# Layer 0 of a two-layer hybrid block: projections and neighbourhood attention as two stages, or as one in two token phases

## The chip, the cores and the metric

The kernel runs on one core of one Trainium2 chip, as one program with one launch. The metric is the device time of one execution in microseconds (us). The kernel before takes 3484.09 us, the median of 3 runs (3483.88 to 3485.11).

## The reference

The block works on 2048 latent tokens and 256 context tokens of 1024 numbers, in float32. Layer 0 is 2-D neighbourhood attention: latent tokens stand on a grid of 32 rows by 64 columns, and each of 16 heads (64 numbers each) lets a query see a window of 8 rows by 16 columns, with a learned bias for the relative position, and all 256 context tokens, in one softmax. Context tokens see the context alone.

```python
h = modulate(x, norm_w, shift, scale)            # rms norm, adaLN
q, k, v, z = jnp.split(h @ w_in, 4, axis=-1)     # w_in: 1024 x 4096
hc = modulate(xc, norm_w, shift_c, scale_c)
qc, kc, vc, zc = jnp.split(hc @ w_in, 4, axis=-1)
s_loc = q . k (window) * dh ** -0.5 + bias       # -inf outside the window
s_ctx = q . k_ctx * dh ** -0.5
p = softmax([s_loc, s_ctx]);  o = p_loc @ v + p_ctx @ v_ctx
x = x + gate * ((o * silu(z)) @ w_out)           # and the same for the context
```

Layer 1 is a gated linear recurrence in both directions, with projections of its own, and a final norm. The change doesn't touch it.

## The kernel before, in words

Full float32 precision is kept by splitting: a number is the sum of a part that the fast float32r product takes (hi) and the exact rest (lo). A projection is three products, hi hi, hi lo and lo hi (`mm3`, L207 to L213).

**Stage 1, `layer0_in`, L216.** The normalised tokens are built transposed and split, in five groups: four of 512 latent tokens and one of 256 context tokens (`GROUPS`). All five stay on chip. The 32 blocks of 128 weight columns (8 each of q, k, v, z; one block is one pair of heads) are loaded once, split by ScalarE and GpSimd, and multiplied with all five groups. q, k and z are written transposed (128 columns of the pair on the partitions, tokens along the row): the weights stand still and 512 tokens stream. Values are wanted with tokens on the partitions: `v_product` holds 128 tokens still and streams 256 value columns (L374). q and k go to DRAM as hi and lo (`split_out`), z with its SiLU (`gate_out`). In the middle, beside the blocks of pairs 1 to 3, stand the bias tables (`bias_tables`, L399) and the sums of adaLN parameters by lanes (`ada_lanes`, `ada_sum`): one of eight sums behind each weight block.

**Stage 2, `attention`, L479.** Pair after pair of heads; of each pair four groups of 8 query rows (`ROWG`; they read 12, 16, 16 and 12 key rows), then the context's queries; of each row group four bands of 16 query columns. I call one pair, row group and band a unit. For a unit and a head: scores into a PSUM tile `s` of two banks (two buffers); VectorE adds the bias table and takes the minimum (L494; scores are kept with their sign turned); ScalarE takes the exponential and its sum (L496); VectorE scales (L499); TensorE transposes in chunks of 128 into `tps` (L509, three banks), which ScalarE, or at each sixth turn VectorE (`EV = "aaaaav"`), copies out (L513, L515); TensorE multiplies with the values of the pair (L522), each head's 64 output rows in one half of the bank `o_ps`; a product of float32 without the split is two instructions in the trace. Scores (L596, L599, L615) stack hi and lo of q on the 128 partitions of one tile (`pair_tile`, L451), and k hi twice or k lo twice under them: two products on 128 rows give all that is wanted. So each of k hi and k lo is loaded twice. Everything is read back from DRAM: q, keys, values (16 loads a pair), tables and z.

**Stage 3, `layer0_out`, L678.** The output projection: both halves of the output weights (64 KB a partition split, `out_weights`) and 18 tiles of 128 tokens. Then layer 1.

**What sets the order.** The program is written for a planner that simulates the engines' times: it orders each engine's instructions beforehand, by what is ready and, among that, by place in the program. `after` adds an order between two instructions of one engine. Nearly all DMAs are issued by SyncE in one order; a tile that takes the place of older tiles waits for those that it overlaps (`reuse_waits="tile"`).

Of the kernel before, what the change touches and what calls it, by code (L numbers as in the profile page):

```python
# [13 lines left out]
ALU = mybir.AluOpType  # L14
# [11 lines left out]
# scores are kept with their sign turned  # L26
# [7 lines left out]
KBLOCKS = [(0, 12), (12, 8), (20, 12)]  # L34
KPARTS = [((0, 0, 12),), ((0, 4, 8), (1, 0, 8)), ((1, 0, 8), (2, 0, 8)), ((2, 0, 12),)]
# [4 lines left out]
TPS = 3  # L40
EV = "aaaaav"
TEB = 6
PB = 4
PCB = 3
# column bands whose context keys are weighted together
# [8 lines left out]
class Core:  # L54
# [71 lines left out]
    def ada_start(self, pool, psum, tag, tag2):  # L126
        """shift and scale of layer 0 from whole rows of weights: shift by lanes, scale on TensorE."""
# [37 lines left out]
    def rsqrt(self, y, x, pool):  # L165
        """y = x ** -0.5 for positive x, by Newton steps from a guess off the exponent."""
# [11 lines left out]
    def norms(self, xts, pool, small, tag="junk"):  # L178
        """1 / rms of the rows of each tile, one column each."""
# [36 lines left out]
    def layer0_in(self):  # L216
        nc, tc, I, S = self.nc, self.tc, self.I, self.S
        with ExitStack() as st:
            pp = st.enter_context(tc.tile_pool(name="l0p", bufs=1, reuse_waits="tile", space=PSUM))

            class PsPool:
                def tile(self, shape, dt, name, tag):
                    return pp.tile(shape, dt, name=name, tag=tag, bufs=4 if tag == "mm" else 3)
            ps = PsPool()
            ha = st.enter_context(tc.tile_pool(name="l0ha", bufs=1, reuse_waits="tile"))
            hi, lo = [], []

            def tokens(pool, g):
                n = GROUPS[g][1]
                hi.append(pool.tile([P, NDC, n], F32R, name=f"hi{g}"))  # L230
                lo.append(pool.tile([P, NDC, n], F32R, name=f"lo{g}"))
            for g in range(3):
                tokens(ha, g)
            wk = st.enter_context(tc.tile_pool(name="l0k", bufs=2, reuse_waits="tile"))
            sx = ExitStack()
            xp = sx.enter_context(tc.tile_pool(name="l0x", bufs=4, reuse_waits="tile", side="right"))
            sm = st.enter_context(tc.tile_pool(name="l0s", bufs=4, reuse_waits="tile"))

            def weights(cg, wh, wl):
                raw = wk.tile([P, NDC, P], F32, name="wraw", tag="wraw", bufs=1)  # L240
                m = nc.sync.dma_start(out=raw, in_=I["w0"][cg])
                if cg in (0, 8, 24):
# [3 lines left out]

            def granule(cg, pool=wk, **kw):
                wh = pool.tile([P, NDC, P], F32R, name="wh", tag="wh", **kw)
                wl = pool.tile([P, NDC, P], F32R, name="wl", tag="wl", **kw)
                weights(cg, wh, wl)  # L250
                return wh, wl

            def split_out(cg, p, t0, n, dst_h, dst_l, keys):
                oh = wk.tile([P, 512], F32R, name="oh", tag="oh")
                ol = wk.tile([P, 512], F32R, name="ol", tag="ol")
                ohv, olv, pv = oh[:, :n], ol[:, :n], p[:, :n]
                if not keys and n == 512:
                    ohv, olv = (custom(t, [[-16, 8], [P, 4], [1, 16]], 7 * 16) for t in (oh, ol))
                    pv = p.rearrange("p (r j c) -> p r j c", r=8, j=4)
                if keys:  # L260
                    nc.scalar.mul(out=ohv, in_=pv, mul=KSCALE)
                    nc.vector.scalar_tensor_tensor(olv, pv, KSCALE, ohv.bitcast(F32), ALU.mult, ALU.subtract)
                else:
                    nc.scalar.copy(out=ohv, in_=pv)
                    nc.vector.tensor_sub(olv, pv, ohv.bitcast(F32))  # L265
                r = slice(cg * P, (cg + 1) * P)
                nc.sync.dma_start(out=dst_h[r, t0:t0 + n], in_=oh[:, :n].bitcast(F32))
                nc.sync.dma_start(out=dst_l[r, t0:t0 + n], in_=ol[:, :n].bitcast(F32))

            def gate_out(cg, p, t0, n):  # L270
                sg = wk.tile([P, 512], F32, name="sg", tag="oh")
                nc.scalar.activation(sg[:, :n], p[:, :n], AF.Sigmoid)
                z = wk.tile([P, 512], F32, name="zo", tag="ol")
                nc.vector.tensor_mul(z[:, :n], p[:, :n], sg[:, :n])
                nc.sync.dma_start(out=S["z"][cg * P:(cg + 1) * P, t0:t0 + n], in_=z[:, :n])

            def q_out(pr):
                return lambda p, t0, n: split_out(pr, p, t0, n, S["qh"], S["ql"], False)

            def k_out(pr):  # L280
                return lambda p, t0, n: split_out(pr, p, t0, n, S["kh"], S["kl"], True)

            def z_out(pr):
                return lambda p, t0, n: gate_out(pr, p, t0, n)

            def x_load(g, xrs):
                t0, n, cond = GROUPS[g]
                for i, xt in enumerate(xrs):
                    src = I["ctx"][i * P:(i + 1) * P, :] if cond else I["x"][t0 + i * P:t0 + (i + 1) * P, :]
                    m = nc.sync.dma_start(out=xt, in_=src)  # L290
                    self.after(m, self.last_dma)
                    self.last_dma = m
                return xrs

            def x_tiles(g):
                return x_load(g, [xp.tile([P, D], F32, name="xt", tag="xt") for _ in range(GROUPS[g][1] // P)])

            def normalise(xrs):
                for i in range(0, len(xrs), 2):
                    rs = self.norms(xrs[i:i + 2], xp, sm)  # L300
# [3 lines left out]
            def build(g, xrs):  # L304
                self.build_hT(xrs, hi[g], lo[g], 0, GROUPS[g][2], 0, HalfPool(xp, 2), ps, "tp", "hf")

            with tc.tile_pool(name="l0a", bufs=1, reuse_waits="tile") as ap:
                self.ada_inputs(ap)
                ada = self.ada_start(ap, ps, "mm", "tp")
                next(ada)  # L310
                x0 = x_load(0, [ap.tile([P, D], F32, name=f"x0{i}") for i in range(4)])
                next(ada)
                self.ada_done(0)
                normalise(x0)
                first = [(granule(0), q_out(0)), (granule(8), k_out(0)), (granule(24, xp, bufs=1), z_out(0))]
                x1 = x_tiles(1)
                build(0, x0)
                next(ada)
            hb = st.enter_context(tc.tile_pool(name="l0hb", bufs=1, reuse_waits="tile"))
            tokens(hb, 3)  # L320
            x2 = [hb.tile([P, 2, D], F32, name=f"x2{i}", tag=f"t4{i}") for i in range(2)]
            x2 = x_load(2, [x2[i // 2][:, i % 2] for i in range(4)])

            def product(w, g, evac):
                t0, n, _ = GROUPS[g]
                wh, wl = w
                p = ps.tile([P, 512], F32, "mm", "mm")
                m = self.mm3(p[:, :n], lambda dc: wh[:, dc, :], lambda dc: wl[:, dc, :],
                             lambda dc: hi[g][:, dc, :], lambda dc: lo[g][:, dc, :])
                evac(p, t0, n)  # L330
                return m

            def token_product(cg, evac):
                w = granule(cg)
                return [product(w, g, evac) for g in range(len(GROUPS))][-1]

            def granules(pr):
                yield token_product(pr, q_out(pr))
                yield token_product(8 + pr, k_out(pr))
                yield token_product(24 + pr, z_out(pr))  # L340

            xs = {1: x1, 2: x2}
            for g in range(len(GROUPS)):
                if g:
                    if g == 4:
# [878 lines left out]
```

## Time and profile before

| | |
|---|---|
| median of 3 runs | 3484.09 us |
| span of the profiled execution | 3477.0 us; its own time with what lies around the span isn't given, and the median run is 7.1 us longer |
| TensorE busy | 3333.7 us, 96% |
| VectorE, ScalarE, GpSimd busy | 57%, 36%, 22% |
| moved by DMA | 424 MB, 122 GB/s |
| stage 1, projections | to 891 us |
| stage 2, attention | 891 to 1607 us |
| stage 3, output projection | 1607 to 1814 us |
| layer 1 | 1814 to 3477 us |

A matmul is recorded with its whole way through the array, so two that follow each other overlap in the records: how dense TensorE is, is read from the distance of their starts. The granted clock of 1.00 is 2.4 GHz, and 0.5 is 1.2 GHz. Names are those of the program: `mm<-hi,wh` writes tile `mm` from `hi` and `wh`.

### The profile page before, as it was taken

Reading aid. Unit: us, or ns where it says so; the run is one execution under the profiler, and the core shown is the slowest. Engines: PE = TensorE matmul, PEld = TensorE weight load, DVE = VectorE, ACT = ScalarE, POOL = GpSimd, SP = SyncE. Lnnn points to the kernel's source line nnn. Section 1 sums busy time; section 2 is a strip of 40 time slices with the busy share of each in tenths; the row PEclk is TensorE's granted clock in tenths of the full one; section 3 lists DMA queues with packets and bytes.
Section 4 is the critical chain, followed back from the end, with each engine's and each line's share of the span. In section 5 each row is a group of like instructions: output and inputs, shape, how many; then the busy total and the mean of one; then the engine's idle time right before and its main releaser. Section 6 shows DMA issues by size and latency. Waiting matters only on the chain. (4 is left out here: it accounts for less than half of the span.)

```text
span 3477.0 us, 57414 instructions
## 1 busy us (share of the span) xinstructions
PE 3333.7 (96%) x22276; PEld 2727.7 (78%) x22276; DVE 1985.4 (57%) x4315; ACT 1261.6 (36%) x2688; POOL 759.9 (22%) x787
## 2 busy tenths in 40 slices
PE   7999999999889999999999999999899999999898
PEld 5778989989667777777888888888778777887687
DVE  7674111111457666675744555555775677777876
ACT  4311110010456666664312333333443344444521
POOL 2210110010012111112322222222342222232321
PEclk9999999999989999999999999999999999999999
DMA  6665232233777778763341111111232333332542
GB/s 234 178 198 186 82 105 77 75 106 112 168 191 180 182 174 189 172 163 99 133 142 43 58 47 55 55 56 55 94 100 78 104 114 115 116 116 98 179 145 106
DMA packets 259880, 424.46 MB, mean 122 GB/s; under 512 B 34956, under 2 KB 138124, under 8 KB 259608
## 3 DMA queue, kind: packets, MB, share of 16 engines
q1 hardware_dynamic: 244824, 372.54, 37.6%
q0 software_dynamic: 14784, 48.25, 3.6%
q8 instruction: 176, 2.88, 0.4%
q14 instruction: 96, 0.79, 0.1%
HBM read 295.22 MB, written 126.96 MB: 121 GB/s over the span
## 5 line engine op out<-in xcount | busy, mean ns | idle before, releaser
L210 PE MATMUL g_ps<-h1h,g_wh 128*128 128x512 f32 x1280 | 517.1, 404 | 5.2 <-DVE qt L984 2.6
L212 PE MATMUL g_ps<-h1h,g_wl 128*128 128x512 f32 x1280 | 516.8, 404 | 0.0
L211 PE MATMUL g_ps<-h1l,g_wh 128*128 128x512 f32 x1280 | 515.3, 403 | 0.0
L210 PE MATMUL mm<-hi,wh 128*128 128x512 f32 (+1 forms) x960 | 351.1, 372 | 5.1 <-DVE ol L265 3.5
L212 PE MATMUL mm<-hi,wl 128*128 128x512 f32 (+1 forms) x960 | 353.8, 370 | 1.8 <-POOL wl L70 1.8
L211 PE MATMUL mm<-lo,wh 128*128 128x512 f32 (+1 forms) x960 | 355.3, 371 | 0.2
L210 PEld LDWEIGHTS g_ps<-h1h,g_wh 128*128 128x128 f32 x1280 | 241.9, 189 | 61.2 <-DVE qt L984 2.9
L212 PEld LDWEIGHTS g_ps<-h1h,g_wl 128*128 128x128 f32 x1280 | 241.8, 189 | 56.0
L211 PEld LDWEIGHTS g_ps<-h1l,g_wh 128*128 128x128 f32 x1280 | 241.7, 189 | 54.0
L496 ACT ACTIVATE p<-p,nm 128x768 f32<-128x768 f32 (+2 forms) x288 | 243.2, 845 | 90.5 <-DVE nm L494 87.0
L70 POOL TENSOR_TENSOR g_wl<-g_raw,g_wh 128x1024 fp32r<-128x1024 f32 x86 | 210.1, 2444 | 292.8 <-ACT g_wh L67 279.9
L509 PE MATMUL tps<-ident,p 128*128 128x128 f32 x1472 | 249.5, 288 | 2.2 <-ACT pc L513 2.0
L818 DVE COPY_PREDICATED pm<-masks,lv 128x256 f32<-128x256 int32 x192 | 85.7, 447 | 271.7 <-PE lv L804 271.5
L509 PEld LDWEIGHTS tps<-ident,p 128*128 128x128 f32 x1472 | 167.0, 144 | 66.8 <-issue 56.7
L210 PEld LDWEIGHTS mm<-hi,wh 128*128 128x128 f32 x960 | 180.2, 189 | 39.4 <-DVE ol L265 4.8
L212 PEld LDWEIGHTS mm<-hi,wl 128*128 128x128 f32 x960 | 181.4, 189 | 33.5 <-POOL wl L70 2.7
L211 PEld LDWEIGHTS mm<-lo,wh 128*128 128x128 f32 x960 | 181.5, 189 | 32.5 <-issue 1.7
L522 PE MATMUL o_ps<-pt,vb 128*64 128x128 f32 x1792 | 176.3, 291 | 25.3 <-DVE ot L562 11.6
L513 ACT COPY pt<-tps 128x512 f32<-128x512 f32 (+2 forms) x283 | 145.8, 515 | 136.5 <-PE tps L509 134.3
L816 ACT COPY km<-k 128x512 f32<-128x512 f32 x192 | 129.3, 673 | 172.0 <-PE lv L804 152.5
L70 POOL TENSOR_TENSOR wl<-wraw,wh 128x1024 fp32r<-128x1024 f32 x24 | 57.5, 2395 | 590.8 <-ACT wh L67 590.8
L761 DVE TENSOR_TENSOR k<-k,F 128x512 f32<-128x512 f32 (+1 forms) x240 | 164.8, 688 | 38.2 <-PE lv L824 33.8
(271 smaller groups left out, 7450.2 us busy)
## 6 DMA issues: line engine op xcount, KB each, us to landing
g_raw<-in_w SPq DMA_DIRECT2D x90, 512.0 KB
wraw<-in_w SPq DMA_DIRECT2D x32, 512.0 KB
adaw<-in_ada_w SPq DMA_DIRECT2D x64, 256.0 KB
vb<-s_v SPq DMA_DIRECT2D x128, 128.0 KB
kh<-s_kh SPq DMA_DIRECT2D x32, 384.0 KB
kl<-s_kl SPq DMA_DIRECT2D x32, 384.0 KB
tabi<-s_ei SPq DMA_DIRECT2D x48, 256.0 KB
s_v<-vo SPq DMA_DIRECT2D x72, 128.0 KB
```

Source lines behind the costliest of these rows:

```text
L70: e_lo.tensor_sub(lo, src, hi.bitcast(F32))
L210: nc.tensor.matmul(ps, wh(dc), hh(dc), start=dc == 0, stop=False)
L211: nc.tensor.matmul(ps, wh(dc), hl(dc), start=False, stop=False)
L212: m = nc.tensor.matmul(ps, wl(dc), hh(dc), start=False, stop=dc == n - 1)
L496: nc.scalar.activation(p[:, :n], p[:, :n], AF.Exp, bias=nm, scale=-1.0, accum_out=sums)
L509: nc.tensor.transpose(ps[:, c, :], p[:, at:at + P], self.ident)
L513: nc.scalar.copy(out=out, in_=ps[:, :n, :])
L522: last[a] = nc.tensor.matmul(o[64 * a:64 * a + 64], values(c, a), ps[a][:, c], start=last[a] is None, stop=end and c == nv - 1)
L761: nc.vector.tensor_mul(kv, kv, kf)
L816: nc.scalar.copy(out=km.rearrange("p (k h i) -> p k h i", h=2, i=b), in_=self.mixed(k2, T, b))
L818: nc.vector.copy_predicated(pm, self.masks[:, j, :].unsqueeze(1).broadcast_to([P, 4, 64]), ps)
```

## The change

`layer0_in` and `attention` become one function, `layer0_mix`.

- **Two phases of tokens.** Two token groups are on chip at a time instead of five. Phase 0 projects the groups 0, 1 and the context for the pairs in turn, and attends to row group 0 and the context's queries; phase 1 projects groups 2 and 3 and attends to the row groups 1 to 3. Weight blocks are loaded and split anew for each phase (80 loads).
- **Mixed by hand in the program's order.** `jobs` yields one product of a weight block with a token group at a time, `attend` one unit at a time, and `mix` lays so many jobs behind each unit. In phase 1 the last pair has no jobs beside it.
- **Scores on 64 rows.** q and k are stored hi and lo in one tensor with a first axis of 2. A head's numbers stay on its own 64 partitions. Scores are three products (hi hi, lo hi, hi lo) on 64 rows, the two heads of the pair in turn, into two PSUM tiles.
- **Values transposed.** Values are projected like q, copied by ScalarE, transposed by TensorE (four chunks of 128) and copied by VectorE; one store.
- **Buffers.** PSUM of the mixed stage: 2 banks for products, 1 for transposes of both kinds, 1 for `o_ps`, 2 score tiles of two banks, one for each head. VectorE takes each third copy of transposed probabilities (`EV = "aav"`).

```diff
-EV = "aaaaav"
+EV = "aav"
-                    first = [(granule(0), q_out(0)), (granule(8), k_out(0)), (granule(24, xp, bufs=1), z_out(0))]
+                    first = [("q", granule(0)), ("k", granule(8)), ("v", granule(16, xp)), ("z", granule(24, xp))]
...
-                        self.mm3(p, lambda dc: hi[g][:, dc, c], lambda dc: lo[g][:, dc, c],
-                                 lambda dc: vh[:, :, dc, :], lambda dc: vl[:, :, dc, :])
-                        vo = vp.tile([P, 2, P], F32, name="vo", tag="vo", bufs=2)
-                        nc.vector.tensor_copy(vo, p)
+            def values_out(pr, p, t0, n, psum, tag):
+                vT = wk.tile([P, 512], F32, name="vT", tag="vT", bufs=1)
+                nc.scalar.copy(out=vT[:, :n], in_=p[:, :n])
+                tp = psum.tile([P, 4, P], F32, name="vtp", tag=tag)
+                m = n // P
+                for c in range(m):
+                    nc.tensor.transpose(tp[:, c, :], vT[:, c * P:(c + 1) * P], self.ident)
+                vo = wk.tile([P, 4, P], F32, name="vo", tag="vo", bufs=1)
+                nc.vector.tensor_copy(vo[:, :m], tp[:, :m])
...
+            class Banks:
+                pp = opened(st, "l0pp", 1, space=PSUM)
+                def tile(self, shape, dt, name, tag):
+                    return self.pp.tile(shape, dt, name=name, tag=tag, bufs=2 if tag == "mm" else 1)
...
+                for i, prev in enumerate(jobs((1, 2), (0, 1, 4))):
+                    if lanes and i % 3 == 2:
                         self.ada_sum(lanes, bp, ps, "tp", prev)
...
-                            for i, off, n in KPARTS[g]:
-                                for h in range(2):
-                                    kv = custom(L["k"][i][h], [[64, n], [1, 32]], a * 64 * KBLOCKS[i][1] + 64 * off + bs)
-                                    nc.tensor.matmul(s[:, at:at + 32 * n], qv, kv, start=h == 0, stop=h == 1)
+                def scores(s, q, parts):
+                    last = [None, None]
+                    for out, kv in parts:
+                        for i, (hq, hk) in enumerate(((0, 0), (1, 0), (0, 1))):
+                            for a in range(2):
+                                m = nc.tensor.matmul(out(s[a]), q(a, hq), kv(a, hk), start=i == 0, stop=i == 2)
+                                if last[a] is not None:
+                                    self.after(m, last[a])
+                                last[a] = m
...
+                                parts.append((lambda t, at=at, m=m: t[:, at:at + 32 * m],
+                                              lambda a, h, kb=kb, off=off, m=m: kb[64 * a:64 * a + 64, h, off:off + m, bs:bs + 32]))
...
+            with ExitStack() as s1:
+                attend = attention(s1, 0)
+                mix([(jobs((3,), (0, 1, 4)), 12)], (attend(0), 5), (attend(1), 5))
+                mix([(jobs((4,), (0, 1, 4)), 12)], (attend(2), 5))
+                mix([(jobs((5,), (0, 1, 4)), 12)], (attend(3), 5))
+                mix([(jobs((6, 7), (0, 4)), 16)], (attend(4), 5))
...
+                    build(2, later(xp, 2), xp, ps, "mm")
+                    mix([(jobs((6, 7), (1,)), 8)], (attend(5), 5))
+                    build(3, later(xp, 3), xp, ps, "mm")
+                    mix([(jobs((0, 1), (2,)), 8)], (attend(6), 5), (attend(7), 5))
+            with ExitStack() as s1:
+                attend = attention(s1, 1)
+                for _ in jobs((0,), (3,)):
+                    pass
+                mix([(jobs((1,), (3,)), 4), (jobs((2,), (2, 3)), 8)], (attend(0), 12), (attend(1), 12))
+                for pr in range(3, 8):
+                    mix([(jobs((pr,), (2, 3)), 8)], (attend(pr - 1), 12))
+                for _ in attend(7):
+                    pass
```

## Rows read from the trace of the kernel before

**Rows 1.** Stages: busy us (instructions) of each engine, granted clock, DMA share, GB/s.
```profile
42.00:350.00 308.00, 296.54 (x1476) 243.59 (x1475) 191.62 (x352) 79.22 (x134) 56.17 (x37) 0.99 0.60 187
...
891.00:1607.00 716.00, 656.84 (x5190) 508.89 (x5189) 480.95 (x1287) 445.28 (x1041) 107.12 (x275) 0.95 0.73 173
1607.00:1814.00 207.00, 205.98 (x943) 169.63 (x943) 115.22 (x182) 47.55 (x80) 71.13 (x43) 1.00 0.42 140
1814.00:2450.00 636.00, 630.49 (x4591) 519.04 (x4590) 353.38 (x672) 213.01 (x394) 166.43 (x142) 1.00 0.17 53
2450.00:3275.00 825.00, 787.62 (x5829) 636.90 (x5828) 589.90 (x1254) 356.97 (x802) 262.62 (x238) 0.98 0.34 109
```

**Rows 2.** TensorE's timeline in the projections: start us, us, instruction.
```profile
611.91 0.39 PE L211 MATMUL mm<-lo,wh 128*128 128x512 f32 x1
612.14 0.39 PE L212 MATMUL mm<-hi,wl 128*128 128x512 f32 x1
...
660.06 0.28 PE L210 MATMUL mmv<-vh,hi 128*128 128x256 f32 x1
660.18 0.28 PE L211 MATMUL mmv<-vl,hi 128*128 128x256 f32 x1
```

**Rows 3.** TensorE's timeline in attention; neighbours of one kind are merged.
```profile
1154.68 0.34 PE L596 MATMUL s<-kl,q 128*128 128x384 f32 x1
1154.86 0.28 PE L599 MATMUL s<-ckh,q 128*128 128x256 f32 x1
...
1213.60 0.28 PE L599 MATMUL s<-ckh,q 128*128 128x256 f32 x1
1213.71 0.28 PE L599 MATMUL s<-ckl,q 128*128 128x256 f32 x1
1213.92 0.98 PE L522 MATMUL o_ps<-pt,vb 128*64 128x128 f32 x13
...
1215.16 0.44 PE L509 MATMUL tps<-ident,p 128*128 128x128 f32 x2
1215.53 1.08 PE L522 MATMUL o_ps<-pc,vc 128*64 128x256 f32 x6
...
1218.53 0.60 PE L509 MATMUL tps<-ident,p 128*128 128x128 f32 x4
```

**Rows 4.** Costliest lines of TensorE in attention: busy, mean ns, idle before, releaser.
```profile
L509 PE MATMUL tps<-ident,p 128*128 128x128 f32 x1472 | 249.5, 288 | 2.2 <-ACT pc L513 2.0
L522 PE MATMUL o_ps<-pt,vb 128*64 128x128 f32 x1792 | 176.3, 291 | 25.3 <-DVE ot L562 11.6 <-DVE ot L560 8.7 <-ACT pt L513 5.0
L596 PE MATMUL s<-kh,q 128*128 128x256 f32 (+1 forms) x384 | 135.4, 366 | 30.0 <-DVE nm L494 29.5 <-DVE zo L274 0.3
```

**Rows 5.** Weight loads of two tiles: duration ns, least, median, most.
```profile
L522 PEld LDWEIGHTS o_ps<-pt,vb x1792: 132/137/232, 905.4 to 1603.0; 128*64 128x64 f32 x200
...
L596 PEld LDWEIGHTS s<-kl,q x384: 186/192/338, 891.5 to 1593.9; 128*128 128x128 f32 x192
```

**Rows 6.** Costliest lines of VectorE and ScalarE in attention.
```profile
L494 DVE CUSTOM_DVE_ANT_0 p<-s,tabi 128x768 f32<-128x768 f32 x128 | 121.8, 952 | 40.1 <-PE tps L509 19.8 <-PE s L599 17.6 <-DMA tabi<-s_ei 2.3
...
L496 ACT ACTIVATE p<-p,nm 128x768 f32<-128x768 f32 (+2 forms) x288 | 243.2, 845 | 90.5 <-DVE nm L494 87.0 <-DVE ars L498 1.8
L513 ACT COPY pt<-tps 128x512 f32<-128x512 f32 (+2 forms) x283 | 145.8, 515 | 136.5 <-PE tps L509 134.3
```

**Rows 7.** The costliest line of VectorE from 42 to 350 us.
```profile
L99 DVE SCALAR_TENSOR_TENSOR adacc<-adaw,sc,adacc 128x512 f32<-128x512 f32 x98 | 75.6, 806 | 43.2 <-DMA adaw<-in_ada_w 42.6
```

**Rows 8.** Output weights: their loads, first and last; timelines of SyncE, ScalarE, GpSimd.
```profile
L634 SPq DMA_DIRECT2D wor<-in_w0o x8: 373/390/541, 1032.6 to 1618.6; - x8
...
1616.29 2.73 SPq L634 DMA_DIRECT2D wor<-in_w0o  x2
...
1619.88 1.05 ACT L67 CAST woh<-wor 128x1024 fp32r<-128x1024 f32 x1 [12.19 <-DMA wor<-in_w0o]
...
1621.00 4.79 POOL L70 TENSOR_TENSOR wol<-wor,woh 128x1024 fp32r<-128x1024 f32 x2 [2.39 <-ACT woh L67]
```

More of the change, by code (lines that the diff above doesn't have):

```diff
@@ L245, in weights, with halves_out @@
                 self.split(wh, wl, raw, nc.scalar, nc.gpsimd)
[L247 to L250, printed above, removed]
                 return wh, wl
[L253 to L259, printed above, removed]
+            def halves_out(name, pr, p, t0, n, keys):
+                t = wk.tile([P, 2, 512], F32R, name="st", tag="st")
+                oh, ol, pv = t[:, 0, :n], t[:, 1, :n], p[:, :n]
@@ L280, in k_out @@
[L280 to L284, printed above, removed]
+                    nc.scalar.mul(out=oh, in_=pv, mul=KSCALE)
+                    nc.vector.scalar_tensor_tensor(ol, pv, KSCALE, oh.bitcast(F32), ALU.mult, ALU.subtract)
+                else:
+                    if n == 512:
+                        oh, ol = (custom(t, [[-16, 8], [P, 4], [1, 16]], 512 * i + 7 * 16) for i in range(2))
+                        pv = p.rearrange("p (r j c) -> p r j c", r=8, j=4)
+                    nc.scalar.copy(out=oh, in_=pv)
+                    nc.vector.tensor_sub(ol, pv, oh.bitcast(F32))
@@ L290, in x_load @@
                     m = nc.sync.dma_start(out=xt, in_=src)
-                    self.after(m, self.last_dma)
-                    self.last_dma = m
-                return xrs
-            def x_tiles(g):
-                return x_load(g, [xp.tile([P, D], F32, name="xt", tag="xt") for _ in range(GROUPS[g][1] // P)])
-            def normalise(xrs):
+                    if self.last_dma is not None:
+                        self.after(m, self.last_dma)
+                        self.last_dma = m
@@ L319, in layer0_in @@
[L319 to L345, printed above, removed]
-                        hi.append(hb.tile([P, NDC, CTX], F32R, name="hi4", tag="t40"))
-                        lo.append(hb.tile([P, NDC, CTX], F32R, name="lo4", tag="t41"))
-                    build(g, xs[g])
-                    if g < 3:
-                        xs[g + 2] = x_tiles(g + 2)
-                        normalise(xs[g + 2])
-                else:
-                    normalise(xs[1])
-                    normalise(xs[2])
-                for w, evac in first:
-                    product(w, g, evac)
@@ new lines, in layer0_mix, with tile, jobs @@
+            self.first_dma, self.last_dma = self.last_dma, None
+            class Banks:
+                pp = opened(st, "l0pp", 1, space=PSUM)
+                def tile(self, shape, dt, name, tag):
+                    return self.pp.tile(shape, dt, name=name, tag=tag, bufs=2 if tag == "mm" else 1)
+            ps = Banks()
+            def jobs(pairs, groups):
+                for pr in pairs:
+                    for kind in "qkvz":
+                        w = granule(KINDS[kind] + pr)
+                        for g in groups:
+                            m = product(kind, pr, w, g, ps, "mm", "tp")
+                            yield m
@@ new lines, in mix @@
+            def mix(work, *att):
+                att = [a for a in att]
+                work = list(work)
+                n, m = sum(k for _, k in work), sum(k for _, k in att)
+                wi, ai = (s for w, _ in work for s in w), (s for a, _ in att for s in a)
+                done = 0
+                for i in range(m):
+                    next(ai, None)
+                    while done * m < (i + 1) * n and next(wi, ai) is not ai:
+                        done += 1
+                for _ in ai:
+                    pass
+                for _ in wi:
+                    pass
@@ new lines, in layer0_mix, with later @@
+            with ExitStack() as s1:
[4 more added lines that the diff above has]
+                mix([(jobs((6, 7), (0, 4)), 16)], (attend(4), 5))
+                sctx.close()
+                def later(pool, g):
+                    xs = x_load(g, [pool.tile([P, D], F32, name="xt", tag="xt", bufs=4) for _ in range(4)])
+                    normalise(xs, pool)
+                    return xs
+                with tc.tile_pool(name="l0x2", bufs=1, reuse_waits="tile", side="right") as xp:
+                    build(2, later(xp, 2), xp, ps, "mm")
+                    mix([(jobs((6, 7), (1,)), 8)], (attend(5), 5))
+                    build(3, later(xp, 3), xp, ps, "mm")
+                    mix([(jobs((0, 1), (2,)), 8)], (attend(6), 5), (attend(7), 5))
@@ L407, in bias_tables @@
             d = sx[col]
[L408 removed]
+            self.after(nc.sync.dma_start(out=bass.AP(tensor=d.tensor, offset=d.offset, ap=[[32, 240], [7680, 16], [1, 32]]), in_=src), self.first_dma)
         for h2 in range(2):
@@ L1189, in tile_kernel @@
     core = Core(ctx, tc, I, out, S)
-    core.layer0_in()
-    core.attention()
+    core.layer0_mix()
     if upto < 2:
```

432 lines of the change are left out of this document (203 added, 229 removed).

## The prediction, made before the change was run

> **What bounds the kernel now.** I read the table of stages first. TensorE is busy in nearly all of every stage but one: layer 0's attention, 891 to 1607 us, where it is busy 656.84 of 716.00 us, at a mean granted clock of 0.95 [rows 1]. So it sits idle there for 59 us. A mean of 0.95 between 1.2 and 2.4 GHz means that about a tenth of the stage, 72 us, ran at 1.2 GHz. In the projections before it only the first 300 us have gaps worth counting (308.00 - 296.54 = 11.5 us), and the output projection behind it has 1 us [rows 1]. VectorE (481 us) and ScalarE (445 us) fill two thirds of the attention stage, DMA 0.73 of it [rows 1]: none of them is the bound, but they share a chain with TensorE (scores, minimum, exponential, scaling, transposes, copies, weighted values). The reader should note how little is idle: laying projections under attention can win 59 us and the slow clock, not more. All else must come from TensorE doing less.
>
> A busy TensorE is not a dense one, so I then read starts, not durations, in its timeline. 512 columns of a projection start 0.23 us apart, 256 columns 0.12 [rows 2]. Scores of 256 columns start 0.12 apart and of 384 columns 0.18 (1154.68 to 1154.86); four transposes take (0.60 - 0.27) / 3 = 0.11 each [rows 3].
>
> **The change, part by part** (us against the profiled execution's span of 3477.0; the median run is 3484.09, and I carry the 7.1 us that lie around the span unchanged).
>
> *Scores.* A unit is one pair of heads, one row group, one band: 8 x 4 x 4 = 128 units, and 16 for the context. Now a head takes two products a part, on 128 rows (halves stacked). A unit of the middle row groups has 2 heads x 6 products x 0.12 = 1.44, of the outer ones 2 x (2 x 0.18 + 2 x 0.12) = 1.20, of the context 0.48: 64 x 1.44 + 64 x 1.20 + 16 x 0.48 = 177. The change makes three products a part on 64 rows, one head above the other. If both run side by side, a unit has 9 x 0.12 = 1.08, 3 x 0.30 = 0.90 or 0.36: 133 in all, -44. If they run one after the other it is 266, +88. No row here has 64-row tiles. The nearest are the weighted values on column halves: 13 products start in 0.98 - 0.27 = 0.71, so 0.059 each and a pair in 0.118, where a lone product of these columns (a transpose) takes 0.11 [rows 3]. Halves overlap there, so I take -44.
> The Trainium skill speaks both ways here. "TensorEngine Tiling (Array Packing)", section Tiling Modes, says that tiles load weights and multiply in parallel, which is -44. "TensorE: Matmul & The Clock Gate", section LDWEIGHTS, says that a load's time goes by columns and not by contraction rows, so that a 64-row load is as dear as a 128-row one, and there are now six in place of four; what that does if loads queue is a rival below.
>
> *Values.* 72 groups x 24 = 1728 products of 256 columns go: 1728 x 0.12 = 207. In come 8 x 4 x 24 = 768 of 512 and 192 of 256 columns (177 + 23) and 144 transposes x 0.11 = 16: +8. Their copies are on ScalarE and VectorE beside the products.
>
> *Mode changes.* A change between whole tiles and halves costs: the last score product starts at 1213.71, the next may start 0.12 later, and the weighted values start at 1213.92: 0.09 [rows 3]. Scores now are in a third mode: one visit a unit, in and out, 144 x 2 x 0.09 = 26, less where scores stand next to weighted values. Ends 0 and 26; I take 18.
>
> *Idle time and clock.* Projections under attention fill the 59: -59. Slow clock: 72 us at half speed did 36 us of work, but part of it is the idle time just counted: ends 0 and -36, taken -25.
>
> *New waits.* The mixed stage is about 1300 us. The recurrence, mixed in the same way, is idle 5.5 of 636 us where projections abound, and 37.4 of 825 later [rows 1]: 0.9% and 4.5%, so 12 to 59. Nearest is the first, since only 24 of 144 units here have few projections: +20.
>
> *The last pair.* Its 12 units have no projection beside them, and transposes now have one bank in place of three, scores one buffer a head. Idle before scores came from VectorE reading them (29.5 of L596's 30.0) [rows 4]. A head's turn needs 0.60 for four transposes, 0.515 for the copy, then about 0.38 and 0.37 for two more: 3.7 a unit, with an exponential of 0.845 in front of a copy now and then [rows 3, 6]. I take 5.8 a unit where TensorE's own work is 4.3: +18. Ends: today's rate, 716 / 136 = 5.3, gives +12; 7.3 gives +36.
>
> *The way out.* Today the first half of the output weights loads at 1032.6, in room that attention leaves free; only the last loads stand at 1618.6 [rows 8]. By the tile sizes of the diff the second phase holds 64 KB of tokens, 32 of weights and outputs and 100 of attention a partition; the fullest stage of before holds about 203. So the 64 KB of output weights come when attention's tables and probabilities are gone. A block takes 3.6 from issue to ScalarE (1616.29 to 1619.88), 1.05 there, 4.79 / 2 = 2.4 on GpSimd [rows 8]. Two of four blocks can be staged; the third follows 3.5 after the end, is split 7.05 later, and the first o tile behind it lands at about 14 and is split at 16. +18, ends 5 and 30.
> The Trainium skill's "SBUF — State Buffer", section Specifications, gives about 208 KiB usable a partition, which would leave those two blocks some 8 KiB; the sum would be the same.
>
> *adaLN and bias tables.* Eight lane sums stand in 24 products (8 x (0.23 x 48 + 0.12 x 24) = 111 us) in place of nine weight blocks of 25 us. VectorE needs 98 x 0.806 for them and waited 43.2 more for their weights [rows 7]: 122 in 111, and TensorE's sums stand in a fixed order. Later projections hide part: +10, ends 0 and 25.
>
> *At nothing.* 80 weight blocks load in place of 32: 48 x 1.05 on ScalarE, 48 x 2.4 = 115 on GpSimd, which is busy 107 of 716 today [rows 1], and 25 MB on queues that carry fewer key bytes per us than now. Uncovered, one block is 3.6 + 1.05 + 2.4 = 7 us against 11 us of products. The copies that move to VectorE (one in three, not one in six) add 0.2 us a unit to about 4.5 of 7.7 [rows 6]. On SyncE loads now queue behind the stores of products; the stretches of one token group (8 blocks of 5.5 us) are the thin place, counted in the waits.
>
> Sum: -44 + 8 + 18 - 59 - 25 + 20 + 18 + 18 + 10 = -36. 3477.0 - 36 = 3441, with the 7.1 around it **3448**.
>
> **Rivals.**
> 1. *The one transpose bank decides (slower).* Each unit turns four times through it, 144 x 4 = 576 turns, and TensorE's order is fixed beforehand: a copy that comes late behind an exponential (0.845) or a weight cast (1.05) stops everything queued behind the transpose, projections too. From a mean stand of 36 / 576 = 0.06 us a turn the gain is gone; at 0.17 us it is 3448 + 98 - 20 (the waits already counted) = 3526. For it: transposes follow in bursts with 0.38 to 0.60 between copies. Against: the recurrence with two such banks loses under 5% [rows 1].
> 2. *Scores don't overlap.* Loads of 64 columns record 137 ns and of 128 columns 192 [rows 5], 55 ns for 64 columns, so 0.11 of pure load for 128. If the two heads' loads queue, a pair takes 0.22 whatever its columns: 64 x 9 x 0.22 + 64 x 6 x 0.22 + 16 x 3 x 0.22 = 222, +45 in place of -44: 3537. By the page's rule on loads (columns alone count) this holds if tiles share one load path; the column halves, whose two loads fit in 0.118, speak against.
> 3. *The seams take it all.* Waits 38, last pair 30, way out 20, adaLN 14 in place of 66: +36, 3484. For it: each end is in the bounds above. Against: all must be high at once.
>
> **How the numbers follow.** Forecast 58%, rival 1 18%, rival 2 12%, rival 3 12%. The forecast's own range, from its terms, is 3395 to 3475 (all low ends together would be -102, all high +81). For 8 in 10 the range takes in rival 1 and stops short of rival 2: 3390 to 3528. What differs by less than 0.2% (7 us) can't be told from no change: faster 0.58, same 0.12, slower 0.30.
>
> **What would show it.** Scores: pairs of starts under 0.02 us apart, then 0.12; rival 2 shows 0.11 between all. TensorE's idle share from 250 us to the output projection under 3%; the clock at 1.0 there. A gap of 15 us or more before the first y product, with the output weights' casts behind the last weighted values. Layer 0 ends near 1570 in place of 1607. Wrong it is if transposes wait for copies by more than 35 us in sum, or if the scores don't fall to about 133 us of starts.

## The result: 9% slower

| | before | after |
|---|---|---|
| median, us | 3483.99 | 3806.97 (3799.27 to 3808.58, 4 runs) |
| ratio | | 1.0929 [1.0914, 1.0944] |
| span of the profiled execution | 3477.0 | 3806.8 |

The forecast was 3448: wrong in sign, and the time lies outside the range. Nearly all of the difference arises ahead of layer 0's output projection. Its first product (the first y product, which writes `y_ps`) starts at 1607.1 us before and at 1931.1 after: 324 of the 330 us by which the two profiled spans differ.

The stages of the changed kernel, in the columns of [rows 1]: until 300 us the first pairs, to 1060 the first token phase, then the second. Its last projection product starts at 1729.8, and the last pair's scores at 1819.1.

```profile
42.00:300.00 258.00, 220.72 (x1105) 180.02 (x1105) 154.08 (x258) 53.87 (x89) 54.91 (x43) 0.91 0.61 184
300.00:700.00 400.00, 385.76 (x2180) 301.18 (x2178) 138.98 (x368) 152.18 (x294) 70.22 (x94) 0.97 0.44 138
700.00:1060.00 360.00, 330.59 (x1570) 247.46 (x1569) 132.59 (x298) 129.58 (x232) 87.91 (x76) 0.87 0.42 127
1060.00:1830.00 770.00, 737.95 (x4691) 557.65 (x4691) 352.25 (x804) 318.24 (x616) 93.90 (x160) 0.99 0.41 120
1830.00:1931.00 101.00, 77.34 (x530) 55.13 (x526) 45.85 (x110) 40.20 (x82) 14.25 (x16) 0.84 0.27 82
...
42.00:1931.10 1889.10, 1752.40 (x10066) 1341.48 (x10065) 823.82 (x1836) 694.16 (x1311) 321.19 (x389) 0.94 0.44 132
```

And the same whole stretch of the kernel before:

```profile
42.00:1607.10 1565.10, 1494.47 (x10016) 1241.84 (x10014) 746.93 (x1779) 581.45 (x1262) 213.25 (x340) 0.98 0.55 148
```

Idle TensorE time did not go away under the projections: it rose from 70.6 to 136.7 us, and the granted clock fell from 0.98 to 0.94, lowest (0.91, 0.87, 0.84) in the three stretches where TensorE stands still for the largest share of the time. The greater part is the 258 us by which TensorE is busy longer, with about the same number of products. A part of these is the clock: its records put 173 us of TensorE's busy time in this stretch at 1.2 GHz, and 57 before. At 1.2 GHz half of such time is lost against 2.4, so the clock costs some 58 us more, as an estimate.

TensorE's timeline of one unit's scores, which answers to [rows 3]:

```profile
1412.73 0.98 PE L429 MATMUL s<-k,q 64*128 64x256 f32 x6 [0.21 <-DVE nm L391]
1413.55 0.52 PE L429 MATMUL s<-kc,q 64*128 64x256 f32 x3
1414.00 0.33 PE L406 MATMUL tps<-ident,p 128*128 128x128 f32 x1
```

Nine products of 64 rows and 256 columns, 0.12 us apart (three in 0.52 - 0.28): no two run side by side. At the ends of the run there is more: the first six take 0.82 us where 0.72 would do, and the transpose stands 0.45 behind the start of the last three where 0.36 would do. The three context products in one piece show why none overlap. They are one head's; the other head's stand elsewhere. The source lists the heads in turn, but each head's products are tied only to their own predecessors, and the planner that fixes TensorE's order took all of one head first.

What TensorE waited for up to 1940 us (us in total, times, longest), and ScalarE's costliest lines from 42 to 1931 us, in the columns of [rows 6]:

```profile
PE mm L209 <- DVE st L257: 21.3, 7, 11.7
PE y_ps L209 <- ACT ohi L66: 18.7, 1, 18.7
PE tps L406 <- ACT pt L410: 17.3, 27, 2.2
PE s L429 <- DVE nm L391: 15.0, 28, 6.8
PE tps L406 <- ACT pc L410: 8.9, 11, 3.3
PE tps L406 <- DVE pc L412: 6.4, 32, 1.0
```

```profile
L393 ACT ACTIVATE p<-p,nm 128x768 f32<-128x768 f32 (+2 forms) x288 | 242.5, 842 | 245.5 <-DVE nm L391 238.2 <-PE o_ps L419 2.2 <-PE mm L210 2.0
...
L264 ACT ACT_TABLE_LOAD x29 | 37.2, 1283 | 9.9 <-PE mm L211 9.5
L393 ACT ACT_TABLE_LOAD x29 | 37.2, 1283 | 4.0 <-DVE nm L391 3.5
```

The last two lines are new: the gate's sigmoid (L264) and the softmax's exponential (L393) now alternate on ScalarE, which loads a function table at each change, 58 times 1.283 us. The kernel before loads one for its sigmoid (L272) and one for its exponential (L496):

```profile
L272 ACT ACT_TABLE_LOAD x1 | 1.3, 1283 | 4.1 <-DVE ol L262 4.1
L496 ACT ACT_TABLE_LOAD x1 | 1.3, 1283 | 5.8 <-DMA s_z<-zo 5.8
```

The way out, in ScalarE's and TensorE's timelines [rows 8]:

```profile
1910.47 1.91 PE L419 MATMUL o_ps<-pc,vc 128*64 128x256 f32 x7
...
1914.85 2.17 ACT L66 CAST woh<-wor 128x1024 fp32r<-128x1024 f32 x2 [6.14 <-DMA wor<-in_w0o]
1923.00 1.04 ACT L66 CAST woh<-wor 128x1024 fp32r<-128x1024 f32 x1 [5.99 <-DMA wor<-in_w0o]
1924.46 1.04 ACT L66 CAST woh<-wor 128x1024 fp32r<-128x1024 f32 x1 [0.41 <-DMA wor<-in_w0o]
1930.17 1.14 ACT L66 CAST ohi<-oraw 128x768 fp32r<-128x768 f32 x2 [4.66 <-DMA oraw<-s_o]
1931.05 0.79 PE L209 MATMUL y_ps<-woh,ohi 128*128 128x512 f32 x1 [18.67 <-ACT ohi L66]
```

### The profile page after: what moved, and what is told of

Its sections match the earlier page's. It is cut to its first block, busy times and chain, and to the rows that moved or that the text cites. A ratio compares the mean times of both kernels' runs of the same rounds, so it can differ in the third digit from the quotient of the medians.

```text
span 3806.8 us, 57510 instructions
## 1 busy us (share of the span) xinstructions
PE 3592.3 (94%) x22324; PEld 2827.5 (74%) x22324; DVE 2066.4 (54%) x4374; ACT 1376.6 (36%) x2741; POOL 868.3 (23%) x835
## 5 line engine op out<-in xcount | busy, mean ns | idle before, releaser
L209 PE MATMUL mm<-hh,wh 128*128 128x512 f32 x1024 | 421.3, 413 | 19.1 <-DVE st L257 9.6
L211 PE MATMUL mm<-hh,wl 128*128 128x512 f32 x1024 | 415.5, 406 | 3.4 <-POOL wl L69 3.4
L210 PE MATMUL mm<-hl,wh 128*128 128x512 f32 x1024 | 412.5, 403 | 0.0
L391 DVE CUSTOM_DVE_ANT_0 p<-s,tab 128x768 f32<-128x768 f32 (+2 forms) x288 | 240.4, 835 | 210.3 <-PE tps L406 168.4
L393 ACT ACTIVATE p<-p,nm 128x768 f32<-128x768 f32 (+2 forms) x288 | 242.5, 842 | 245.5 <-DVE nm L391 238.2
L69 POOL TENSOR_TENSOR wl<-wraw,wh 128x1024 fp32r<-128x1024 f32 x80 | 192.7, 2409 | 574.7 <-ACT wh L66 556.6
L429 PE MATMUL s<-k,q 64*128 64x256 f32 (+1 forms) x1152 | 239.3, 335 | 16.5 <-DVE nm L391 14.8
L209 PEld LDWEIGHTS mm<-hh,wh 128*128 128x128 f32 x1024 | 198.6, 194 | 75.7 <-DVE st L257 10.0
L211 PEld LDWEIGHTS mm<-hh,wl 128*128 128x128 f32 x1024 | 197.9, 193 | 53.3 <-issue 5.0
L210 PEld LDWEIGHTS mm<-hl,wh 128*128 128x128 f32 x1024 | 198.7, 194 | 43.0 <-issue 4.4
L429 PEld LDWEIGHTS s<-k,q 64*128 64x128 f32 x1152 | 166.6, 193 | 71.3 <-DVE nm L391 39.4
```

Of the source, the lines that this page charges most:

```text
L69: e_lo.tensor_sub(lo, src, hi.bitcast(F32))
L209: nc.tensor.matmul(ps, wh(dc), hh(dc), start=dc == 0, stop=False)
L210: nc.tensor.matmul(ps, wh(dc), hl(dc), start=False, stop=False)
L211: m = nc.tensor.matmul(ps, wl(dc), hh(dc), start=False, stop=dc == n - 1)
L391: nc.vector.tensor_tensor_reduce(p[:, :n], sview, table, 1.0, 3.0e38, ALU.add, ALU.min, nm)
L393: nc.scalar.activation(p[:, :n], p[:, :n], AF.Exp, bias=nm, scale=-1.0, accum_out=sums)
```

## The experiments

Each ratio is against runs of the kernel before on the same chip. The edits below are given in short form, not line by line.

| run | median us | ratio, 95% interval |
|---|---|---|
| e1 scores padded with zeros | 3722.30 | 1.0696 [1.0677, 1.0715] |
| e2 scores stacked as before | 3717.11 | 1.0680 [1.0655, 1.0704] |
| e3 before, 64-row scores | 3557.81 | 1.0226 [1.0205, 1.0247] |
| e4 heads in turn | 3737.01 | 1.0733 [1.0716, 1.0751] |
| **e5 before, 64-row scores, heads in turn** | **3456.98** | **0.9928 [0.9912, 0.9943]** |
| e6 gate by exponential | 3861.50 | 1.1083 [1.1061, 1.1105] |
| e7 two transpose banks | 3768.99 | 1.0823 [1.0805, 1.0841] |
| e8 no sigmoid | 3764.17 | 1.0813 [1.0794, 1.0831] |
| e9 = e4 + two transpose banks in phase two | 3634.51 | 1.0451 [1.0435, 1.0466] |
| e10 8 buffers for summed weights | 3759.44 | 1.0803 [1.0786, 1.0821] |
| e11 before, one transpose bank | 3610.97 | 1.0376 [1.0361, 1.0392] |
| e12 = e9 + e10 | 3607.45 | 1.0366 [1.0350, 1.0381] |
| e13 = e12, no sigmoid | 3594.06 | 1.0335 [1.0317, 1.0352] |

### p1: products alone

> The disputed cost by itself: a kernel of TensorE products only, in an order held fixed, all of 256 columns; it computes nothing of the reference. Sequences of 24: whole products (128 rows, 128 columns of weights), products of 64 rows with the two row halves in turn into two banks, and products of 64 weight columns with the two column halves in turn, in float32r, float32 and bfloat16; then runs of 8, 4 and 2 whole products alternating with as many 64-row or 64-column ones. Theory A (64-row tiles of float32r run one after another, and a change of the kind of tile has a price of its own): the float32r 64-row products stand as far apart as whole ones, 0.12 us, and the shorter the runs, the longer the same work: about 0.19 us for each change from whole to part and back. Rival B (the prediction's step: the two halves run side by side, and what the kernel lost came from elsewhere): 0.06 to 0.07 us apart on the mean, and a change below 0.1 us.

```diff
+for i in range(n):   # rows; the whole and column products alike
+    a = i % 2
+    matmul(bank[a][:, :256], t[64*a:64*a+64, 0:128], t[64*a:64*a+64, 512:768])
```

TensorE's timeline, first the sequences of 24, then whole and 64-row products in runs of 8 and of 2:

```profile
47.88 1.69 PE L53 MATMUL rows_r<-xr 64*128 64x256 f32 x24
49.50 3.13 PE L45 MATMUL full_r<-xr 128*128 128x256 f32 x24
52.56 5.40 PE L61 MATMUL cols_f<-xf 128*64 128x256 f32 x48
...
109.49 1.21 PE L45 MATMUL rf_r<-xr 128*128 128x256 f32 x8
110.62 0.74 PE L53 MATMUL rr_r<-xr 64*128 64x256 f32 x8
111.29 1.21 PE L45 MATMUL rf_r<-xr 128*128 128x256 f32 x8
...
213.28 0.50 PE L45 MATMUL rf_r<-xr 128*128 128x256 f32 x2
213.71 0.39 PE L53 MATMUL rr_r<-xr 64*128 64x256 f32 x2
214.03 0.50 PE L45 MATMUL rf_r<-xr 128*128 128x256 f32 x2
```

Read starts: 24 half products take 49.50 - 47.88 = 1.62 us, 24 whole ones 3.06. The halves do run side by side, in float32r too, so Theory A is wrong there and the forecast's step right. With the price of a change it is the other way round. But a there-and-back of 8 + 8 takes 1.80 and of 2 + 2 takes 0.75: (1.80 - 0.75) / 6 = 0.175 a pair of products, and 0.75 - 2 x 0.175 = 0.40 is left, 0.2 us for each change, as Theory A had it (0.19). The prediction's 0.09 is the gap at the last product alone; as much again is lost on the first one behind the change, as in the changed kernel's rows above (0.09 and 0.10). The Trainium skill's "TensorEngine Tiling (Array Packing)", section Tiling Modes, says both things, that tiles run in parallel and that a change of the mode drains TensorE; it gives no price, and the trace does.

### e1, e2: whole score products in the changed kernel

> The changed kernel with each head's queries set among zeros on all 128 rows (the other head's 64 rows are zero), so the scores are as many products as in it, three a part, but whole ones; the key tiles stay. To make room the tables have 7 buffers in the second phase, the values 4 and the context turns 3. Theory A (the changes between whole products and 64-row products have a price, about 0.19 us each, some 540 of them more than before): 3807 - 100 = 3705 us (3680 to 3740). Rival B (TensorE's extra work hides in its waits; the one transpose bank and the copies set the pace): 3790 to 3815. Rival C (the 64-row products cost by their number alone, changes are free): 3800 as well, but the next kernel falls.

> The changed kernel with the scores as before: the high and low halves of a head's keys stacked on 128 rows, its queries in both row halves, two whole products a part in place of three of 64 rows; the same buffers as the zero-padded one. All else (one stage, two phases, transposed values) stays. Theory A (score products 2016 to 1344, -88 us, and some 540 changes fewer, -100): 3807 - 188 = 3620 us (3580 to 3660). Rival B (waits decide): 3780 to 3815. Rival C (number of products alone): 3807 - 88 = 3720.

```diff
 e1:
-q(a, h) = q[64*a:64*a+64, h]        # k likewise
+q(a, h) = q[:, a, h]                # other head's rows are zero; k[:, h]
 e2:
-for i, (hq, hk) in enumerate(((0, 0), (1, 0), (0, 1))):
+for h in range(2):                  # keys' halves stacked, queries twice
```

Counted in the traces up to the first y product, changes between kinds of tile (whole, 64 rows, 64 columns; the few products of the adaLN sums left out) are 607 before, 1146 after, 580 in e1 and e2. e1 gives back 85 us of the 566 x 0.2 = 113, with no product fewer: changes have a price, and Rival C, whose number e2 happens to meet, falls. The 85 is not the price alone, since e1's TensorE also stands still for 24 us more and has a better clock (0.97 in place of 0.94):

```profile
42.00:1848.20 1806.20, 1645.77 (x10064) 1308.97 (x10063) 837.39 (x1836) 691.66 (x1311) 392.49 (x469) 0.97 0.48 138
42.00:1842.20 1800.20, 1588.06 (x9395) 1231.02 (x9393) 833.92 (x1837) 690.28 (x1311) 320.73 (x389) 0.95 0.55 149
```

e2 (the second line) has 672 products fewer than e1 and gains 5 us, not 88: TensorE is busy 58 us less and idle 52 more. What it no longer computes it waits, so Theory A missed e2 by 97. The same view as above of e2's waits:

```profile
PE tps L406 <- ACT pt L410: 43.1, 42, 3.9
PE s L429 <- DVE nm L391: 29.2, 36, 14.8
PE mm L209 <- DVE st L257: 22.9, 8, 12.4
```

Transposes wait for the copy that empties their only bank, so TensorE's own work was no longer the only bound.

### e3, e5, e4: 64-row scores alone, and the heads in turn

> The kernel before with this one part of the change: queries and keys stay on their head's own 64 rows, three products a part, the two heads in turn, both heads' scores ahead of their softmaxes. The separate projection stage and the values' products stay. Theory A (672 more products at 0.12 to 0.18 us, one after another, and about 550 more changes at 0.19): 3484 + 88 + 105 = 3677 us (3620 to 3720). The prediction's step (side by side): 3484 - 44 + 15 = 3455. Rival C (number alone): 3572. If it stays under 3520, the loss is in the merging of the stages and not in the scores.

> The kernel before with 64-row scores as in the earlier run, and the two heads chained in turn. Theory A: the scores fall from 263 to some 135 us; the earlier run had only 27 us of TensorE waits over 0.15 us from 42 us to the first product of the way out, the kernel before 89; with less work to cover them they come back: 3558 - 128 + 60 = 3490 us (3430 to 3515). The prediction's step alone (no waits): 3484 - 44 + 18 = 3458. Rival B (no overlap in place): 3558.

> The changed kernel with one more order: the products of the two heads of a pair are chained in turn (head 0, head 1, head 0, ...), where the changed kernel's order on TensorE holds all products of one head and then all of the other. Theory A (side by side works as in the product-only kernel, 61 ns apart, when the halves stand in turn; it was the order that kept it from happening): the scores fall from 263 to some 135 us of TensorE; of those 128 us the waits take back a part, as the stacked form showed (-88 us of products, -5 us of time): 3760 us (3680 to 3795), with the starts in pairs in the trace. Rival B (with keys read in strides and sums kept open the halves don't overlap): starts stay 0.12 us apart, 3807 us.

```diff
 e5, e4:
-if last[a] is not None: after(m, last[a])   # each head's own order (e3)
+if last is not None: after(m, last)         # one order for both heads
```

One unit of e5 on TensorE, and its stretch up to the first y product at 1572.7 us:

```profile
1205.34 1.00 PE L533 MATMUL s<-k,q 64*128 64x256 f32 x12
1206.18 0.52 PE L533 MATMUL s<-ck,q 64*128 64x256 f32 x6
1206.63 0.44 PE L509 MATMUL tps<-ident,p 128*128 128x128 f32 x2
```

```profile
42.00:1572.70 1530.70, 1504.12 (x10694) 1207.16 (x10692) 754.17 (x1780) 571.66 (x1260) 202.97 (x340) 0.99 0.46 139
```

Twelve products in 0.84 us, 0.07 each. By order alone the same products differ by 101 us: e3 is 2% slower than before, e5 0.7% faster. e3 was expected at 3677 and came out 119 lower. Of these the traces show 54 as idle time up to the first y product, 71 us before and 16 in e3:

```profile
42.00:1674.70 1632.70, 1616.30 (x10693) 1306.95 (x10691) 759.32 (x1780) 587.64 (x1260) 206.73 (x340) 0.99 0.43 130
```

Both heads' scores now stand ahead of their softmaxes, which would fill the waits of [rows 4]; that this is the reason wasn't tried by itself. Changes are 421 more than before, not the 550 expected (25 us at 0.19). The rest is open.

In e5 idle time is 1530.7 - 1504.1 = 27. The starts inside its score runs, waits left out, add up to some 132 us against some 172 before (-40), there are 938 - 607 = 331 more changes (+66 by p1's price) and 44 less idle time: -18. The clock records give another -18, since only 22 us of TensorE's busy time stand at 1.2 GHz in place of 57. Together that is close to the 34 us by which the stretch is shorter; the kernel as a whole gains 25, and why some of it is lost again behind the stretch is open. In the changed kernel turns give 70 us (e4); most of the rest of the 128 went into waits, as in e2: idle time rises by 64. e5 beats both kernels. e4 stands 280 us above it: that is what merging the stages costs with all that came with it (banks, buffers, transposed values).

### e7, e9, e11: banks for transposes

> The changed kernel with PSUM divided the other way: two banks for transposes, one for the projections' products. Theory A (one transpose bank costs what TensorE's transposes wait for copies, 36 us in the changed kernel's trace; a projection's copies take about 1 us and can be covered by attention): 3780 us (3760 to 3830, a loss if the projections now wait). Rival B (the one bank sets the pace, the forecast's first rival): under 3740.

> The changed kernel with the two heads' score products in turn, and in the second phase two banks for transposes and one for projections; the first phase keeps one and two. Theory A (with two banks there the waits of TensorE in the second phase go: with the banks divided so throughout, the stretch from 1060 to 1789 us had 0.8 us of waits over 0.15 us, against 90 in the kernel with turns alone): 3737 - 75 = 3660 us (3640 to 3690). Rival B (the projections' one bank gives it back, or the softmax chain is what transposes wait for): 3715 to 3740.

> The kernel before with one bank for the attention's transposes in place of three, nothing else. It asks what one bank costs where no projection is at hand to cover: each head's second turn waits for the copy of its first (0.52 us for four chunks, 0.37 for two, in the trace before) unless scores or weighted products stand between. Theory A (a cost of 0.1 us or more on each of 576 turns): 3484 + 60 = 3545 us (3515 to 3600). Rival B (the order on TensorE covers it): 3480 to 3500.

```diff
 e7 (e9: from the second phase on):
-bufs=2 if tag == "mm" else 1
+bufs=2 if tag == "tp" else 1
 e11:
-TPS = 3
+TPS = 1
```

The waits of e11, then the second phase of e4, e9 and e7 in the columns of [rows 1]:

```profile
PE tps L509 <- ACT pt L513: 80.8, 141, 7.5
```

```profile
1060.00:1760.00 700.00, 634.38 (x4416) 458.61 (x4417) 337.73 (x763) 294.65 (x579) 84.66 (x151) 0.98 0.42 125
```

```profile
1060.00:1660.00 600.00, 589.48 (x4165) 436.98 (x4162) 307.33 (x688) 271.42 (x530) 86.06 (x139) 0.99 0.46 135
```

```profile
42.00:300.00 258.00, 199.61 (x982) 161.98 (x980) 148.41 (x252) 49.19 (x82) 44.81 (x29) 0.89 0.56 171
1060.00:1788.00 728.00, 727.39 (x4711) 564.65 (x4710) 344.98 (x785) 317.69 (x607) 94.77 (x159) 1.00 0.43 129
```

One bank in place of three costs the kernel before 132 us (e11), twice what Theory A gave: 132 / 576 = 0.23 us a turn. With projections beside it, two banks in the second phase take the run 102 us down (e9). The two stretches shown are not quite alike: idle time is 66 us of 700 in e4 and 11 of 600 in e9, but e4's last 100 us hold next to no projections; in its first 600 idle time is 53. How far the projections run ahead goes with the banks: of the 2016 score products the changed kernel and e4 have 396 left behind the last projection product, about the last two pairs' attention, and e9 has 215, about the last pair's. Two banks throughout gain 38 (e7): the second phase has no idle time, but with one bank for projections the first stretch waits 58 us in place of 37.

### e6, e8, e10: tables and summed weights

> The changed kernel with the gate's sigmoid made of the exponential that the softmax uses, 1 / (1 + exp(-z)), two more VectorE operations on each of 36 tiles; ScalarE then has no function table to load between gate and softmax. The changed kernel's trace has 58 such loads of 1.283 us in the stage (74 us of ScalarE), the kernel before 2. Theory A (each load stands between a softmax and the copies that free the one transpose bank): about half of it comes back, 3807 - 40 = 3767 us (3740 to 3785). Rival B (ScalarE is idle two thirds of the time, the loads are hidden): 3800 to 3810.

> The changed kernel with the gate's sigmoid left out: ScalarE copies the product there instead (so the gate is z squared and the output not the reference's), all else the same. ScalarE then loads no function table between gate and softmax; the form with an exponential had cost VectorE 121 us of reciprocals (3.03 us each) and told nothing of the loads. Theory A (58 loads of 1.283 us, some of them in front of a copy that frees the one transpose bank): 3807 - 30 = 3777 us (3755 to 3795). Rival B (ScalarE is idle two thirds of the time, the loads are hidden): 3800 to 3812.

> The changed kernel with 8 buffers in place of 2 for the weights that VectorE sums while the first pairs are projected. From 42 to 300 us TensorE waits 50 us in the changed kernel (17 in the kernel before), 21 of them for copies of products that stand behind those sums on VectorE, which waits 41 us for the weights. Theory A (the sums hold VectorE up): 3807 - 25 = 3782 us (3770 to 3797). Rival B (the weights of the projections come late on SP's queue, and more loads ahead of them make it later): 3805 to 3830.

```diff
 e6:
-activation(sg, p, Sigmoid)
+activation(sg, p, Exp, scale=-1.0); sg = sg + 1; sg = reciprocal(sg)
 e8:
+copy(out=sg, in_=p)                 # in the sigmoid's place
 e10:
-w = pool.tile([P, 512], F32, name="adaw", tag="adaw")             # 2 buffers
+w = pool.tile([P, 512], F32, name="adaw", tag="adaw", bufs=8)
```

e6 settles nothing: its reciprocals put 121 us more on VectorE, in the chain that TensorE waits for.

```profile
L266 DVE RECIPROCAL zst<-zst 128x512 f32<-128x512 f32 (+1 forms) x40 | 121.1, 3029 | 0.9
```

e8 loads one table in these stages in place of 59; ScalarE's other work is the same, and it gains 43 us: more than half of the 74 us of loads was on the path. That exponential and sigmoid load from different table sets, and that a set is the unit to batch by, is in the Trainium skill's "ScalarE: Activation LUTs", section Table sets: the hidden batching unit; the traces agree, at 1.283 us a load. e10 gains 48; what 8 buffers would give the kernel before, whose sums waited as long [rows 7], wasn't tried. VectorE's sums waited for weights in the changed kernel (the same line as [rows 7]):

```profile
DVE adacc L98 <- DMA adaw<-in_ada_w: 41.5, 36, 3.1
```

and with 8 buffers TensorE is busy 18 us more until 300 us:

```profile
42.00:300.00 258.00, 239.18 (x1265) 197.13 (x1264) 163.59 (x285) 63.09 (x108) 56.98 (x49) 0.97 0.66 210
```

### e12, e13: do the causes add up?

> The changed kernel with three of the causes found put right together: the heads' score products in turn, two transpose banks in the second phase, 8 buffers for the summed weights. Theory A (the causes add up): 3634.5 - 45 = 3590 us (3575 to 3605). Rival B (they overlap: what one gives another had already covered): 3610 to 3635.

> The same, with the gate's sigmoid left out as well (a copy in its place, so the output is not the reference's), which takes the function table loads away. Theory A: 3590 - 40 = 3550 us (3530 to 3570); what is then left of the distance to the kernel before with the scores in turn (3457) is about 90 us: the first phase's one bank, some 16 us more on the way out, 7 of values. Rival B (the loads are hidden once the second phase has two banks): 3580 to 3595.

```profile
42.00:1712.90 1670.90, 1573.31 (x10068) 1189.16 (x10066) 821.86 (x1837) 611.12 (x1253) 316.48 (x389) 0.97 0.49 149
```

Not in full. On top of e9 the buffers give 27 (48 alone) and the tables 13 (43 alone; the intervals of e12 and e13 just touch): what one cure gives, another had partly covered. e13, above, still stands 137 us over e5. Of that the traces show 71 as idle time (1670.9 - 1573.3 = 97.6 against 27; 20 of it the way out), 8 as values, and 1063 changes against 938, 25 by p1's price. Some 33 is left, with a clock of 0.97 against 0.99. The clock records put 54 us of TensorE's busy time at 1.2 GHz against 22, which is 16 of the 33 as an estimate; the rest is open.

## Why the prediction was wrong, step by step

- **Scores: the step that failed first.** The mechanism and its size were right (p1; -40 in e5) but it hung on the two heads standing next to each other in TensorE's queue, and I read that off the source. The planner's order put it at the step's other bound: +88 in place of -44. That order on TensorE alone decides it, e3 and e5 show.
- **Mode changes: mis-sized.** I took 18 from one extra visit a unit at 0.09. There are 539 more, since each head's scores are a visit and projections come between, and a change costs 0.2 (p1): some 108 us as an estimate. e1, which takes 566 changes away, gives back 85.
- **Idle time, clock and new waits (-59, -25, +20): failed.** Idle time rose by 66, and the clock fell, which by its records costs some 58 us more where 25 less was taken. I carried the recurrence's waits over, a stage with two transpose banks. Rival 1 named the cause and nearly its threshold: transposes wait 41 us in the changed kernel, 0.07 a turn, and the sign "more than 35 us" was passed. What I missed is that the waits shown are what is left when TensorE is slow for other reasons: each time a cure made it faster (e2, e4), they came back.
- **At nothing: failed.** Moving the gate beside the softmax issues 58 table loads where the two stages had 2. A listing of each engine's functions per stage would have shown it; 43 us alone (e8).
- **adaLN: too small.** +10 taken; 48 come back with more buffers (e10).
- **The last pair: too small.** Its 12 units take 93 us (1819.1 to 1912.4), 7.8 each in place of 5.8, though TensorE waits for only some 6 of the 93: its own pace was slower, with scores one after another, more changes and a clock of 0.91. And it is not alone: the pair before it has no projections beside it either, which the sum didn't have.
- **Right:** values (+8; by starts, waits left out, some 789 us of projections and 16 of transposes in place of 797) and the way out (+18; the y product waits 18.7). Of the way out the third block's cast stands 10.6 us behind the last product (1923.0, 1912.4), as in the sum (3.5 + 7.05).
- **Rival 2** looks confirmed, since products stand 0.12 apart, but p1 refutes its mechanism. **Rival 3** named places that did cost (adaLN, the last pair, the way out), but not the scores, the changes or the tables.

Taken one by one, scores (+88), changes (+108), idle time (+66), clock (+58) and values (+8) come to 328 us, where 324 were lost ahead of the first y product. That is an estimate and not a proof of each part: e1 changes the clock and the waits along with the changes, and e12 and e13 show that cures overlap. The tables and adaLN make waits, so they stand in these terms and not beside them.

## What to carry to other kernels

Where a gain needs two instructions to be neighbours in a queue, order them by hand and look at the starts; the same 2016 products cost or won by that alone. Before merging two stages, list what each holds alone (PSUM banks, function tables, buffers that an engine waits on in order): the merged stage pays for every one that they must now share, and an engine that is 92% busy has little to win in return.

## What the runs showed of the hardware

- Two 64-row float32r products on different row halves start 4 ns apart when neighbours (p1), and 24 take 1.62 us against 3.06 whole. Neighbours on the same half stand 0.12 us apart (the changed kernel).
- A change between whole and 64-row products costs about 0.2 us, half of it behind the change (p1).
- Sigmoid and exponential don't share a ScalarE table: 1.283 us at each alternation (the changed kernel).
- A reciprocal of 128x512 takes VectorE 3.35 us, where the minimum pass over 128x768 takes 0.95 (e6; the 3.03 in the line shown mixes in eight smaller tiles).
